# Hybrid decoder layer on one core: two moving operands of gate and up in memory of their own, decode columns kept in SBUF, output projection's tiles in shared buffers

## The chip, the cores and the metric

The kernel runs on one core of one Trainium2 chip. The metric is the device time of one execution in microseconds. The core has a matrix engine (PE), a vector engine (DVE), a scalar engine (ACT), a general engine (POOL) and a sequencer that issues DMAs (SP). Each engine works through its own list of instructions in order, and waits at an instruction until what it needs is there. POOL issues DMAs too.

## The reference

One inference step of one layer with 2048 prompt rows and 8 decode rows of width 1024. Two head groups (sliding-window attention and gated linear attention) give `mix`; then come the output projection, an RMS norm and a gated feed-forward layer:

```python
D_MODEL, SEQ, DEC_BATCH = 1024, 2048, 8
D_FF = 2816

def rmsnorm(x, g):
    r = lax.rsqrt(jnp.mean(x * x, axis=-1, keepdims=True) + EPS)
    return x * r * g

def finish(x, o_attn, o_gla, r_gla, ...):
    ...
    h = x + jnp.concatenate([o_attn, g], axis=-1) @ w_o
    z = rmsnorm(h, ffn_norm_g)
    return h + (jax.nn.silu(z @ w_gate) * (z @ w_up)) @ w_down
```

`finish` is called for the prompt rows and for the decode rows. All is float32.

## The kernel before

A float32 matrix is held as two halves, high and low, each of a type that PE multiplies at full rate. `split` (L91) makes them: a copy to the rounded type on ACT (L92), and the rest by a subtraction on DVE (L93). `mm3` (L102) multiplies two split matrices with three matmuls (L104, L105, L106), high by high, high by low, low by high.

The program runs through these stages:

- Projections, attention and gated linear attention, up to about 765 us. The last blocks of linear attention (L800 to L889) store `mix_d` blocks from SP (L889) and the final state (L948). The change doesn't touch this code.
- The output projection, from about 740 to 947 us (L963 to L1080). It goes over sixteen tiles of 128 prompt rows and then the eight decode rows. The prompt has two halves of 1024 rows, 0 and 1 (`sb`), with eight tiles each; a pair of tiles 4 apart belongs together (`mt` 0 to 3), so the order is 0, 4, 1, 5, 2, 6, 3, 7, 8, 12, 9, 13, 10, 14, 11, 15, decode.
- Gate and up, in two passes over the weights, one for each half of the prompt (959 to 1403 and 1403 to 1847 us). Each pass goes over eleven pairs of weight blocks of 256 columns.
- The down projection, from 1853 us to the end (L1246 to L1347).

For a tile, `load_tile` fetches the tile of `mix_d` (`mr`, L995) and of x (`h`, L1000), and splits `mr` into `mt`. `product` multiplies by the two halves of W_o, `WO0` and `WO1` (48 matmuls into `ps_wo`), adds to h on DVE (`add_h`, L580), and stores h (L1022) for the end of the layer. `normalise` follows one tile later: Square with a sum on ACT (L1030), the root (L111 on DVE, L112 on POOL), the scaled z on DVE (L1032), eight transposes on PE (`ps_zT`, L1037), and the copies of the result into four tiles b11, b21, b12, b22 (L1040). When a pair of tiles is done, `operands` builds the seven moving operands of Strassen's scheme (in Winograd's form) from them: four differences on DVE (L958), seven splits (`zhl`, a ring of three buffers), and seven stores from POOL into DRAM, `zc_d` (L1057). The scheme replaces eight block products with seven, P1 to P7.

The eight decode rows ride along as four extra columns (eight rows in two blocks of four) on the last pair, (half 1, `mt` 3): their normed rows are copied into columns 128 to 131 of that pair's b tiles (L1043), so its operands are 132 columns per block wide and can be built only when the decode rows have been through the output projection. In half 1 the moving operands are therefore 516 wide, and a unit of products is run in two pieces of 258.

Gate and up take the seven operands of a half as z0 to z6, loaded on SP (L1242), in the order P1, P6, P2, P7, P5, P4, P3 (`PRODS`). The tiles of all seven lie in one pool that is opened when the output projection's pools are closed. For each pair of weight blocks the raw weights come from DRAM (`wrg`, L1179), sums and differences of blocks are made on DVE (L958, L961: `sx`, `sy`), and the results are split (`whl`). A unit is one product for gate or up: twelve matmuls of 128x512 in half 0. Their results meet in `ps_a` (P1, P2), `ps_b` (P6, P7, P4) and `ps_c` (P5, P3). At the end of a pair the result's seven operands for the down stage go to DRAM from POOL (`md_d`, L1236).

What sets the order: the program is written in Python, and before it is built, a scheduler that simulates the engines chooses for each engine the order of its instructions, among those that dependencies and buffers allow. Pools are stacks of memory; a tile that is opened over a closed one waits until the older tiles' last users are done.

## Time and profile before

| | us |
|---|---|
| runs shown, median (lowest to highest) | 2315.32 (2309.81 to 2316.54) |
| the profiled execution | 2311.51 |
| its span in the trace | 2309.7 |
| PE busy in the span | 2227.1 |
| last product of a prompt tile with W_o ends | about 937.8 |
| first product of gate and up begins | 959.10 |
| first P5 product of gate and up begins | 996.34 |

Times in the profile are counted from the start of the span. A line of the timeline gives the start, the duration, the engine, the kernel's line, the operation with its output and input tiles, and in brackets how long the engine stood idle before it and for what. A line of the waits view gives an engine's waits by cause: total, number and the longest. A line of the windows view gives for a stretch its length, each engine's busy time with its number of instructions in the order PE, PEld, DVE, ACT, POOL, then the clock granted to PE, the DMA engines' busy share, and GB/s.

### The profile page before, as it was taken

To read this page: it belongs to the slowest core of one execution; us is meant where nothing else is said; L and a number is where in the kernel's file an instruction comes from. 1 tells how busy PE (TensorE), PEld (TensorE's weight loads), DVE (VectorE), ACT (ScalarE), POOL (GpSimd) and SP (SyncE) were. 2 spreads that over 40 slices of the span, in tenths; PEclk is the share of its full clock that TensorE was granted. 3 is DMA by queue.
4 is the path that set the end of the run, shared out by engine and by line. 5 is a ranking of instruction groups with operands and counts; after the bars stand their busy time and mean duration, and the time that the engine had idled before them with its cause. 6 is when DMAs were issued, how large, how long until landed. Compare 5 with 4: busy or idle time off the path is not lost.

```text
span 2309.7 us, 34809 instructions
## 1 busy us (share of the span) xinstructions
PE 2227.1 (96%) x12649; PEld 1923.6 (83%) x12649; DVE 1600.5 (69%) x3236; ACT 957.2 (41%) x2120; POOL 623.8 (27%) x791
## 2 busy tenths in 40 slices
PE   8999998999999999699999999999999989999998
PEld 6888886788887788578888889999999968787887
DVE  6787887587776567556666666767676674847477
ACT  5676777343443234323232333333333243535342
POOL 2443434365465133201111110101010122222222
PEclk9999998999998999899999999999999999999999
DMA  7323234245325689872324257323233277878877
GB/s 239 122 75 115 93 108 153 90 157 165 126 87 214 225 275 288 276 247 87 119 79 127 78 177 290 110 84 115 87 111 97 83 225 171 210 165 213 185 184 263
DMA packets 204935, 364.57 MB, mean 158 GB/s; under 512 B 15411, under 2 KB 128332, under 8 KB 200780
## 3 DMA queue, kind: packets, MB, share of 16 engines
q1 hardware_dynamic: 167740, 258.80, 34.2%
q0 software_dynamic: 37024, 103.55, 17.9%
q8 instruction: 100, 1.64, 0.3%
q14 instruction: 71, 0.58, 0.1%
HBM read 211.09 MB, written 152.27 MB: 157 GB/s over the span
## 4 chain that ended last, share of the span: by engine, by line
PE 31%; issue 20%; POOL 5%; DMA 1%; DVE 0%; POOLq 0%; ACT 0%; SPq 0%; DVEq 0%; ACTq 0%
PE ps_b L105 4%; PE ps_b L104 4%; PE ps_b L106 4%; POOL h_d L1329 4%; PE ps_c L105 3%; PE ps_c L104 3%; PE ps_c L106 3%; PE ps_a L105 3%; PE ps_a L106 3%; PE ps_a L104 3%; POOL out_y_prompt_dram L1324 1%; DMA z<-zc_d_P 1%; POOL md_d L1236 1%; DMA zc_d_P<-zhl 0%; DMA wrg<-in_w_gate_dram 0%
## 5 line engine op out<-in xcount | busy, mean ns | idle before, releaser
L104 PE MATMUL ps_b<-z,whl 128*128 128x258 f32 (+1 forms) x792 | 253.8, 321 | 3.2 <-DMA z<-zc_d_P 3.2
L105 PE MATMUL ps_b<-z,whl 128*128 128x258 f32 (+1 forms) x792 | 254.0, 321 | 0.0
L106 PE MATMUL ps_b<-z,whl 128*128 128x258 f32 (+1 forms) x792 | 252.8, 319 | 0.0
L92 ACT CAST dm<-mr 128x384 fp32r<-128x384 f32 (+1 forms) x224 | 108.0, 488 | 188.4 <-PE ps_b L106 97.6
L104 PE MATMUL ps_a<-z,whl 128*128 128x258 f32 (+1 forms) x528 | 170.9, 324 | 8.3 <-DMA z<-zc_d_P 8.3
L105 PE MATMUL ps_a<-z,whl 128*128 128x258 f32 (+1 forms) x528 | 170.7, 323 | 0.0
L106 PE MATMUL ps_a<-z,whl 128*128 128x258 f32 (+1 forms) x528 | 170.3, 323 | 0.0
L104 PE MATMUL ps_c<-z,whl 128*128 128x258 f32 (+1 forms) x528 | 168.6, 319 | 0.9 <-DMA z<-zc_d_P 0.9
L105 PE MATMUL ps_c<-z,whl 128*128 128x258 f32 (+1 forms) x528 | 169.1, 320 | 0.0
L106 PE MATMUL ps_c<-z,whl 128*128 128x258 f32 (+1 forms) x528 | 168.9, 320 | 0.0
L104 PEld LDWEIGHTS ps_b<-z,whl 128*128 128x128 f32 x792 | 149.3, 189 | 15.9 <-DMA z<-zc_d_P 3.5
L106 PEld LDWEIGHTS ps_b<-z,whl 128*128 128x128 f32 x792 | 149.2, 188 | 12.1
L105 PEld LDWEIGHTS ps_b<-z,whl 128*128 128x128 f32 x792 | 149.2, 188 | 11.9
L93 DVE TENSOR_TENSOR dm<-mr,dm 128x384 fp32r<-128x384 f32 (+1 forms) x224 | 114.9, 519 | 59.4 <-ACT dm L92 59.4
L92 ACT CAST whl<-wrg 128x512 fp32r<-128x512 f32 x132 | 81.6, 620 | 150.5 <-PE ps_b L106 81.2
L802 POOL TENSOR_TENSOR bd<-E,qTb 64x128 f32<-64x128 f32 x224 | 127.1, 567 | 60.6 <-ACT E L787 47.2
L93 DVE TENSOR_TENSOR whl<-wrg,whl 128x512 fp32r<-128x512 f32 x132 | 90.9, 688 | 42.9 <-ACT whl L92 42.7
L961 DVE TENSOR_TENSOR gu<-ps_c,gu 128x512 f32<-128x512 f32 (+1 forms) x130 | 77.9, 600 | 61.0 <-PE ps_c L106 60.3
L1236 POOL DMA_DIRECT2D md_d<-m x22 | 15.7, 713 | 373.7 <-DVE m L1199 360.3
L104 PEld LDWEIGHTS ps_a<-z,whl 128*128 128x128 f32 x528 | 100.8, 191 | 17.0 <-issue 4.4
L104 PEld LDWEIGHTS ps_c<-z,whl 128*128 128x128 f32 x528 | 99.8, 189 | 9.3 <-ACT whl L92 1.3
L105 PEld LDWEIGHTS ps_a<-z,whl 128*128 128x128 f32 x528 | 100.5, 190 | 8.2
(385 smaller groups left out, 6625.9 us busy)
## 6 DMA issues: line engine op xcount, KB each, us to landing
mr<-md_d SPq DMA_DIRECT2D x24, 1344.0 KB
zc_d_P<-zhl POOLq DMA_DIRECT2D x49, 512.0 KB, 6.1
wrg<-in_w_gate_dram SPq DMA_DIRECT2D x44, 512.0 KB
wrg<-in_w_up_dram SPq DMA_DIRECT2D x44, 512.0 KB
nT_d<-nT SPq DMA_DIRECT2D x16, 1024.0 KB
zT<-nT_d SPq DMA_DIRECT2D x8, 2048.0 KB
z<-zc_d_P SPq DMA_DIRECT2D x7, 2064.0 KB
z<-zc_d_P SPq DMA_DIRECT2D x7, 2048.0 KB
```

What stands on the lines that cost most here:

```text
L92: nc.scalar.copy(h, src)
L93: (eng or nc.vector).tensor_tensor(l, src, h.bitcast(F32), ALU.subtract)
L104: nc.tensor.matmul(ps, lh, rh, start=start, stop=False, skip_group_check=more)
L105: nc.tensor.matmul(ps, lh, rl, start=False, stop=False, skip_group_check=more)
L106: nc.tensor.matmul(ps, ll, rh, start=False, stop=stop, skip_group_check=more)
L802: nc.gpsimd.tensor_tensor(bv[rows, :, h], eo, qo, ALU.mult)
L961: nc.vector.tensor_tensor(out, a, b, ALU.add)
L1236: nc.gpsimd.dma_start(md_d[sb][g][:, :, q, fp - GROUPS[g][0], :], src.rearrange("p (m t) -> p m t", m=4))
L1324: nc.gpsimd.dma_start(O["y_prompt"][0, ti * P:(ti + 1) * P, cols], hq[which])
L1329: nc.gpsimd.dma_start(h_d[ti][:, cols], c, accum_op=ALU.add)
```

## The change

Memory is laid out anew around the output projection:

- z0 and z1 (P1 and P6) get pools of their own, opened before the output projection. z2 and z3 lie over WO0, z4 and z5 over WO1, z6 over the `mt` tiles; for this each half of W_o has a pool of its own, padded.
- To make room, h tiles come from the ring of seven buffers `cu` that later holds the weight splits (`whl`), the differences t1 to t4 from `csum`, the pool that later holds weight sums; z, b11 to b22 are single instead of double; the first two `mr` tiles use the memory of z0 and z1.
- The decode rows no longer ride on the last pair's DRAM operands. They are normed into a small tile `zd`, their seven operands are built in it by the same differences (`sums_z`), and split into `zdec` in SBUF. In half 1 seven copies on POOL (L1275) put them into columns 512 to 515 of z0 to z6, whose loads now bring 512 columns. `operands` of the last pair follows tile 15. Four of its seven splits use two `mt` buffers (`zhl2`) beside the ring of three.
- The decode rows' h is stored from POOL instead of SP (L1032).
- The pool of gate and up's results is divided in two, with the same number of buffers.

```diff
+    zdec = pool(ctx, "c_zdec", 1).tile([P, 7, 2, 16], F32R, name="zdec")
...
+    zph = ctx.enter_context(ExitStack())
+    zpools = {q: pool(zph, f"g_z{q}", 1, side="right") for q in (0, 1)}
+
+    def ztile(q, name):
+        return zpools[q].tile([P, 2, 4, 516], F32R, tag="z", name=name)
...
+        wops = [pool(ph, f"m_wo{dh}", 1, side="right") for dh in range(2)]
         mixp = pool(ph, "m_mix", 2, side="right")
-        wop = pool(ph, "m_wo", 1, side="right")
         hlp = pool(ph, "m_hl", 3, side="right")
-        hp = pool(ph, "m_h", 3, side="right")
-        zp = pool(ph, "m_z", 2, side="right")
+        zp = pool(ph, "m_z", 1, side="right")
         bp = pool(ph, "m_b", 1, side="right")
-        tp = pool(ph, "m_t", 1, side="right")
...
-            h = hp.tile([P, D], F32, tag="h", name="h")
+            h = cu.tile([P, D], F32, tag="hl", name="h")
...
-                mr = hlp.tile([P, 1056], F32, tag="hl", name="mr")[:, :1024]
+                mr = ztile(tiles.index(ti), "mr").rearrange("p s k t -> p (s k t)")[:, :1024].bitcast(F32)
...
-            nc.sync.dma_start(h_d[ti] if ti < NB else hdec_d, h[:n])
+            if ti < NB:
+                nc.sync.dma_start(h_d[ti], h)
+            else:
+                nc.gpsimd.dma_start(hdec_d, h[:n])
...
+            t = [csum.tile([P, 512], F32, tag="s", name=f"t{i}").rearrange("p (k t) -> p k t", k=4) for i in range(4)]
+            sums_z(b, t)
+            spare = []
+            for q, src in enumerate((b11, t[1], b21, t[2], t[0], t[3], b22)):
+                if (sb, mt) == (1, 3) and q >= 3:
+
+                    if not spare:
+                        two = mixp.tile([P, 2 * KD * P + 16], F32R, tag="mix", name="zhl2")[:, :2 * KD * P]
+                        spare = [x for x in two.rearrange("p (i s k t) -> i p s k t", i=2, s=2, k=4)]
+                    hl = spare.pop(0)
+                else:
+                    hl = hlp.tile([P, 2, 4, P], F32R, tag="hl", name="zhl")
+                split(hl[:, 0], hl[:, 1], src)
+                nc.gpsimd.dma_start(zc_d[sb][q][:, :, :, mt * P:mt * P + P], hl.bitcast(F32))
...
             if ti == NB:
-                normalise(ti, hs.pop(ti), [x[:, :, P:P + 4] for x in bs[1, 3]])
-                operands(1, 3, bs.pop((1, 3)))
+
+                d = bp.tile([P, 8, 4, 4], F32, name="zd")
+                b = [d[:, i] for i in (0, 2, 7, 6)]
+                normalise(ti, hs.pop(ti), b)
+                sums_z(b, [d[:, i] for i in (4, 1, 3, 5)])
+                split(zdec[:, :, 0], zdec[:, :, 1], d[:, 0:7].rearrange("p q k t -> p q (k t)"))
                 return
...
-            if j == 1 and (sb, mt) != (1, 3):
+            if j == 1:
                 operands(sb, mt, bs.pop((sb, mt)))
...
-                bs[ti // 8, ti % 4] = [bp.tile([P, 4, 132], F32, tag=f"b{q}", name=f"b{q}", bufs=2) for q in range(4)]
+                bs[ti // 8, ti % 4] = [bp.tile([P, 4, P], F32, tag=f"b{q}", name=f"b{q}") for q in range(4)]
...
-        zcp = pool(ph, "g_zc", 1, side="right")
+        for q in range(2, 7):
+            zpools[q] = pool(ph, f"g_z{q}", 1, side="right")
...
-            zc = {name: zcp.tile([P, 2, 4, 516], F32R, tag=f"z{q}", name=f"z{q}")[:, :, :, :WIDTHS[sb]]
-                  for q, name in reversed(list(enumerate(PRODS)))}
+            zc = {name: ztile(q, f"z{q}") for q, name in enumerate(PRODS)}
             for q, name in enumerate(PRODS):
-                nc.sync.dma_start(zc[name].bitcast(F32), zc_d[sb][q])
+                nc.sync.dma_start(zc[name][:, :, :, 0:512].bitcast(F32), zc_d[sb][q])
+                if sb == 1:
+                    nc.gpsimd.tensor_copy(zc[name][:, :, :, 512:516],
+                                          zdec[:, q].bitcast(F32).rearrange("p s (k t) -> p s k t", k=4))
```

How this moves instructions is shown at three places. A row has the line, the operation, the output and input tiles (the number behind a name tells its instances apart) and the shape; "x4" counts equal rows. In lines of the changed kernel L1212 is the weight load, L1273 the z load, L1030 the store of h.

SP's list from the end of the output projection on, before: seven z loads in a row behind the store of the decode rows, and weight loads of the second pair behind them.

```order
L1022 DMA h_d11_4834<-h_9762 128x1024
L1179 DMA wrg_10473<-in_w_gate_dram 128x4x256
L1022 DMA h_d15_4838<-h_9846 128x1024
L1022 DMA hdec_d_4839<-h_9962 8x1024
L1242 DMA z0_10184<-zc_d0_P1_4840 128x8x512
L1242 DMA z1_10183<-zc_d0_P6_4841 128x8x512
L1242 DMA z2_10182<-zc_d0_P2_4842 128x8x512
```

SP's list of the changed kernel, from the store of tile 8's h on, and again from that of tile 15's on:

```order
L1030 DMA h_d8_4831<-h_9169 128x1024
L1273 DMA z0_10204<-zc_d0_P1_4840 128x8x512
L1002 DMA mr_9770<-mix_d11_84 128x1024
L1007 DMA h_9853<-in_x_prompt_dram 128x1024
L1030 DMA h_d12_4835<-h_9253 128x1024
L1273 DMA z1_10205<-zc_d0_P6_4841 128x8x512
```

```order
L1030 DMA h_d15_4838<-h_9853 128x1024
L1273 DMA z2_10206<-zc_d0_P2_4842 128x8x512
L1273 DMA z3_10207<-zc_d0_P7_4843 128x8x512
L1273 DMA z4_10208<-zc_d0_P5_4844 128x8x512
L1273 DMA z5_10209<-zc_d0_P4_4845 128x8x512
L1212 DMA wrg_10499<-in_w_gate_dram 128x4x256
```

z0 stands eight prompt tiles earlier, behind the store of tile 8, and z1 behind that of tile 12; z2 to z5 stand behind the store of tile 15 and no longer behind that of the decode rows.

ACT's list around the Square of tile 15, before. The tiles `zhl` are splits of the operands of the pair of tiles 10 and 14, `whl` are weight splits of the first pair of gate and up, and z_10076 belongs to tile 15.

```order
L92 CAST whl_10266<-sy_10263 128x512
L92 CAST whl_10283<-wrg_10201 128x512
L92 CAST whl_10299<-wrg_10205 128x512
L92 CAST whl_10315<-sx_10241 128x512
L1040 COPY b3_9645<-ps_zT_9920 128x4x128
L1030 ACTIVATE z_10017,ss_10018<-h_9762 128x1024
L92 CAST zhl_9938<-t1_9927 128x4x128
L92 CAST zhl_9942<-b1_9643 128x4x128
L92 CAST zhl_9946<-t2_9928 128x4x128
L92 CAST zhl_9950<-t0_9926 128x4x128
L1030 ACTIVATE z_10076,ss_10077<-h_9846 128x1024
```

ACT's list at the same place in the changed kernel, where z_10083 belongs to tile 15, z_10138 to the decode rows, and zhl_10111 and zhl2_10123 to the operands of the last pair:

```order
L92 CAST zhl_9953<-t2_9935 128x512
L92 CAST zhl_9957<-t0_9933 128x512
L92 CAST zhl_9961<-t3_9936 128x512
L92 CAST zhl_9965<-b3_9652 128x512
L1051 COPY b1_9850<-ps_zT_10038 128x512
L1041 ACTIVATE z_10083,ss_10084<-h_9853 128x1024
L92 CAST zhl_10111<-b0_9849 128x512
L1051 COPY b3_9852<-ps_zT_10097 128x512
L1041 ACTIVATE z_10138,ss_10139<-h_9969 8x1024
L92 CAST zhl2_10123<-t0_10103 128x512
```

The Square of tile 15 stands behind all seven splits of the pair before, not behind five of them, and only two weight splits stand ahead of it (whl_10233 and whl_10250, further up in the list) instead of seven. On PE the decode rows' transposes, which stood ahead of the first product of gate and up, stand behind its first 24 (the two units of P1).

SP's list at the start of the output projection in the changed kernel (h_8493, h_8509 and h_8569 are the x tiles 0, 4 and 1; mr_8570 is the mix tile 1):

```order
L948 DMA out_gla_state_prompt_dram<-Sbd_4981 64x128 x4
L889 DMA mix_d15_88<-mob_8412 128x512
L1007 DMA h_8493<-in_x_prompt_dram 128x1024
L1007 DMA h_8509<-in_x_prompt_dram 128x1024
L1002 DMA mr_8570<-mix_d1_74 128x1024
L1007 DMA h_8569<-in_x_prompt_dram 128x1024
```

Before, the x tiles 0, 4 and 1 stood ahead of the state's stores, and the mix tile 1 stood right behind the last mix store (L889). Correspondingly DVE adds `ps_wo` to the first two tiles (four additions) only behind the last work of the linear attention, ahead of the scaled z of tile 0.

More of the change, by code (lines that the diff above doesn't have):

```diff
@@ L1043, in normalise, with sums_z @@
                         nc.vector.tensor_copy(bs[2 * j + hf], pv[:, :, 4 * j:4 * j + 4])
-        def operands(sb, mt, b):
-            w = 132 if (sb, mt) == (1, 3) else P
-            b11, b21, b12, b22 = (x[:, :, :w] for x in b)
-            t1, t2, t3, t4 = (tp.tile([P, 4, 132], F32, tag=f"t{i}", name=f"t{i}")[:, :, :w] for i in range(4))
+        def sums_z(b, t):
+            b11, b21, b12, b22 = b
+            t1, t2, t3, t4 = t
             sub(t1, b12, b11)
@@ L1080, in hymba_kernel, with out @@
         after(tiles[-1])
-    cy = pool(ctx, "c_out", 2)
+    cy1, cy2 = pool(ctx, "c_out1", 2), pool(ctx, "c_out2", 2)
+    def out(tag, name):
+        return (cy2 if tag in ("gu3", "uu2", "uu3") else cy1).tile([P, 516], F32, tag=tag, name=name)
     def units(parts, sums):
@@ L1134, in __init__ @@
             self.pp, self.pieces, self.done = ppool, pieces, done
-            self.p1, self.u2, self.u3 = (cy.tile([P, 516], F32, tag=tag + x, name=tag + x) for x in ("p1", "u2", "u3"))
+            self.p1, self.u2, self.u3 = (out(tag + x, tag + x) for x in ("p1", "u2", "u3"))
             self.banks = {}
```

29 lines of the change are left out of this document (14 added, 15 removed).

## The prediction

> **What bounds the kernel now.** I read the page first, for the engine that is busy throughout.
>
> ```profile
> PE 2227.1 (96%) x12649; PEld 1923.6 (83%) x12649; DVE 1600.5 (69%) x3236; ACT 957.2 (41%) x2120; POOL 623.8 (27%) x791
> PE   8999998999999999699999999999999989999998
> ```
>
> TensorE is busy for 96% of the span, and the change removes none of its products: it can only win idle time of PE, or matmuls at half clock. The row of tenths has one hole worth the name, the seventeenth slice, which reads 6 (16 to 17 fortieths of 2309.7: 924 to 982 us). So I read next what PE waited for.
>
> ```profile
> PE ps_zT L1037 <- DVE z L1032: 6.9, 1, 6.9
> PE ps_a L104 <- DMA z<-zc_d_P: 8.3, 2, 4.3
> PE ps_b L104 <- DMA z<-zc_d_P: 3.2, 2, 3.0
> PE ps_c L104 <- DMA z<-zc_d_P: 0.9, 1, 0.9
> PE ps_wo L104 <- ACT mt L92: 4.2, 2, 3.0
> ```
>
> The first four lie at one place, the step from the output projection to gate and up: 6.9+8.3+3.2+0.9 = 19.3 us of idle time. One is for the decode rows' norm (z of L1032), the others for the moving operands z0 to z6 out of DRAM. The last line is the start of the output projection. The windows of 10 us show the hole with its clock (after the engines: PEclk, DMA share, GB/s):
>
> ```profile
> 930.00:940.00 10.00, 10.00 (x50) 7.91 (x49) 7.97 (x13) 2.24 (x6) 3.43 (x4) 1.00 0.60 184
> 950.00:960.00 10.00, 1.89 (x10) 1.73 (x11) 6.57 (x14) 2.94 (x5) 2.43 (x4) 0.56 0.84 297
> 960.00:970.00 10.00, 7.60 (x23) 5.59 (x22) 1.37 (x2) 1.26 (x2) 1.56 (x2) 0.75 1.03 328
> ...
> 1000.00:1010.00 10.00, 10.00 (x45) 8.09 (x44) 2.41 (x5) 1.85 (x3) 0.71 (x1) 1.00 1.02 358
> ```
>
> PE is full up to 940 and again from 1000. Between them it stands, and where it runs the clock is down, to 0.56 and 0.75 of full speed, while the DMA share is over 1: the transfers set the pace. The timeline gives the order of events:
>
> ```profile
> 945.90 1.03 PE L1037 MATMUL ps_zT<-ident,z 128*128 128x128 f32 x8
> 950.34 0.29 SPq L1022 DMA_DIRECT2D hdec_d<-h  x1
> 950.81 40.70 SPq L1242 DMA_DIRECT2D z<-zc_d_P  x7
> 953.83 0.99 PE L1037 MATMUL ps_zT<-ident,z 8*128 8x8 f32 x8 [6.90 <-DVE z L1032]
> 959.10 0.80 PE L104 MATMUL ps_a<-z,whl 128*128 128x512 f32 x1 [4.28 <-DMA z<-zc_d_P]
> 964.81 0.46 PE L105 MATMUL ps_a<-z,whl 128*128 128x512 f32 x1
> 965.34 0.40 PE L104 MATMUL ps_a<-z,whl 128*128 128x512 f32 x1
> 967.20 0.40 PE L106 MATMUL ps_a<-z,whl 128*128 128x512 f32 x1
> 970.62 0.51 PE L104 MATMUL ps_b<-z,whl 128*128 128x512 f32 x1 [3.02 <-DMA z<-zc_d_P]
> 982.03 0.76 PE L104 MATMUL ps_a<-z,whl 128*128 128x512 f32 x1 [4.03 <-DMA z<-zc_d_P]
> 996.34 0.47 PE L104 MATMUL ps_c<-z,whl 128*128 128x512 f32 x1 [0.93 <-DMA z<-zc_d_P]
> ```
>
> The seven loads (2 MB each) start only at 950.8, behind the decode rows' store on SP, and PE meets z0, z1, z2 and z4 before they are there. At full clock a product starts every 0.2325 us (965.34 to 967.20, eight steps); after the wait of 4.28 it is 0.43 (from 959.10 thirteen steps to 964.81, 0.44 on the mean). From the end of tile 15's transposes (946.93) to the first P5 product at 996.34 are 49.4 us. The work in them is the decode transposes, 0.99, and eight units of twelve products (P1, P6, P2, P7, gate and up), 96 × 0.2325 = 22.3. So **26 us are lost here**: some 19 idle, the rest half clock. Nothing else in the profile is open to this change.
>
> **The change, part by part.** (1) *The step to gate and up.* z0 and z1 are loaded when the first two tiles of half 1 (8 and 12) are done, tens of us before they are wanted, and z2 to z5 as soon as the last products with each half of W_o are done (942 and 946, by the decode products that end at 946.0), no longer behind the decode norm. The decode transposes move behind the 24 P1 products. All seven z waits should go. What is late next is the chain that feeds it. Its rows of before:
>
> ```profile
> 938.39 7.67 PE L1019 MATMUL ps_wo<-WO,mixdec 128*40 128x512 f32 x32
> 939.92 0.62 ACT L92 CAST zhl<-t 128x512 fp32r<-128x512 f32 x1 [5.80 <-DMA zc_d_P<-zhl]
> 940.45 1.05 ACT L1030 ACTIVATE z<-h 128x1024 f32<-128x1024 f32 x1
> 944.30 1.28 DVE L1032 SCALAR_TENSOR_TENSOR z<-h,rs_r,gBf 128x1024 f32<-128x1024 f32 x1
> 945.64 0.62 ACT L92 CAST zhl<-b 128x512 fp32r<-128x512 f32 x1 [1.99 <-DMA zc_d_P<-zhl]
> 952.41 1.27 DVE L1032 SCALAR_TENSOR_TENSOR z<-h,rs_r,gBf 8x1024 f32<-8x1024 f32 x1 [0.74 <-POOL rs_r L112]
> ACT zhl L92 <- DMA zc_d_P<-zhl: 70.1, 26, 6.6
> ```
>
> and, from the page's groups, what one split of weights takes on ACT and on DVE:
>
> ```profile
> L92 ACT CAST whl<-wrg 128x512 fp32r<-128x512 f32 x132 | 81.6, 620 | 150.5 <-PE ps_b L106 81.2
> L93 DVE TENSOR_TENSOR whl<-wrg,whl 128x512 fp32r<-128x512 f32 x132 | 90.9, 688 | 42.9 <-ACT whl L92 42.7
> ```
>
> In the new ACT order the Square of tile 15 (940.45 before) stands behind all seven splits of the pair before, of which the last ran at 945.64 because three buffers turn with the stores' landing. So Square starts near 946.3; from Square to the transposes took 945.90 − 940.45 = 5.45 us, of which some 1.5 was queueing on DVE and POOL: I take 950.1 for the transposes, **4.2 us of idle time that was not there**. The 24 P1 products then run to about 957. The decode norm starts after the copy of tile 15's b (951.7); its Square, rstd and z take what they took before (from 950.34, when the rows were complete, to 953.68, 3.3 us), and on DVE four differences, one weight sum and two splits of 0.7 stand among them: transposes at about 960, **some 3 us idle**. Then P6 needs its weight split, which in the new DVE order comes behind the decode copies and all splits of tile 15's operands; of the fourteen weight splits of the first pair only two are made ahead (before, the four in the ACT rows of the last section as well, and the three ahead of them). At 0.62 (ACT) and 0.69 (DVE) each (the last two rows) I make it ready at 964 to 965: **4 to 5 us idle**. From there DVE (sums and splits, some 1.4 us a unit) is faster than PE (2.8 a unit), and z6 is not wanted before P3. Sum of idle: 4.2+3+4.5 = 11.7. Half clock after waits of this length: before, 13 products at 0.44 after 4.28 us is 13 × 0.2 = 2.7 us lost. Two such spells would be 5, but what is lost while a feeder is late is no loss of its own: I take 2 to 3. Left: 14 of 26. **Gain 12 us**, bounds 5 (every wait half as long again, 20 idle and half clock) and 20 (only the first wait of 4.2 left, with its half clock).
>
> On the clock the Trainium skill (TensorE: Matmul & The Clock Gate, Part 1: The HAM clock gate) says that an idle window of about 3.4 us throttles PE to half, and that about 3.4 us of work free it. The trace agrees for the 4.28 us wait (half clock for 5.7 us). By that rule the wait of 3 us might go free and the two others cost about 1.7 each, 3.4 together instead of my 2 to 3.
>
> (2) *Start of the output projection.* The first h tiles come from a ring that still holds other things, so in the new SP order their loads stand behind the mix store of the last block, and ahead of the second pair's mr.
>
> ```profile
> 765.26 0.32 SPq L889 DMA_DIRECT2D mix_d<-mob  x1
> 765.69 2.50 SPq L995 DMA_DIRECT2D mr<-mix_d  x3
> 767.76 1.04 PE L1037 MATMUL ps_zT<-ident,z 128*128 128x128 f32 x8
> 771.82 0.50 PE L104 MATMUL ps_wo<-WO,mt 128*128 128x512 f32 x1 [3.02 <-ACT mt L92]
> ...
> PE ps_wo L106 <- DVE mt L93: 1.1, 1, 1.1
> ```
>
> Before, tile 0's transposes ran at 767.76, in a gap; now h lands after about 768, four adds of 0.69, Square, rstd and z follow, and the transposes come at about 773.5, but into the wait for mt that PE has anyway (771.82), shifted by the two loads' issue, 0.7. I take **+1**. Bounds: −1 (the 1.1 us wait for the low half of mt goes, since its split now stands ahead of the block's own work) and +5 (an h load takes the 6.1 us that mr took from 765.69 to the product, and then the adds).
>
> (3) *The output projection's stream.* z0 and z1 put 4 MB more on the DMA engines between some 870 and 930.
>
> ```profile
> 780.00:940.00 160.00, 160.00 (x759) 132.97 (x758) 107.77 (x162) 60.71 (x101) 47.61 (x58) 1.00 0.86 268
> ```
>
> PE has no idle time in these 160 us, at a DMA share of 0.86; 4.2 MB at the 358 GB/s of the window from 1000 take 11.7 us of 60, against 0.14 × 60 = 8.4 free. So the stores of the operands land a little later, and with them the splits (their waits stand above, 70.1 us in 26). Single instead of double b, z and difference tiles hang on the same splits: b22 is free after the last of seven, some 7 × 2.9 (939.92 to 945.64, two steps) = 20 us into a pair of tiles, which takes PE 2 × 12.1 = 24 (48 products at 0.23 and the transposes, 1.03). **+0.5**, bounds 0 and +5.
>
> (4) *The rest at 0.* Seven POOL copies of decode columns (high and low halves of 16 columns) lie between md_d stores on an engine that is busy for 27%. Only the second piece of a unit needs its copy; bounds 0 and +3, if a copy waits for its z and holds a store. Loads of 2 KB runs at the start of half 1: PE has no gap there.
>
> ```profile
> 1390.00:1400.00 10.00, 10.00 (x45) 8.09 (x44) 8.47 (x14) 3.50 (x6) 0.71 (x1) 1.00 1.01 428
> ```
>
> The operands of the last pair are now 512 wide, not 528, and no longer wait for the decode rows: in part 1. The down stage loads its first operands after the last gate product as before.
>
> **Sum:** −12 + 1 + 0.5 = −10.5 on the profiled execution's 2311.5 (span 2309.7 and 1.8 around it): 2301. That execution lies 3.8 below the median of the runs shown and 1.7 above the lowest, so I put the median at **2302**.
>
> **Rivals.** *All of it* (0.20): the chain keeps up, because splits and sums fill ACT and DVE idle time (DVE is busy 6.6 and 1.4 of 10 us in the windows at 950 and 960); only tile 15's late transposes stay: −20 + 1, about 2293 (with the 1 us of the median). *The stall changes its name* (0.20): PE waits as long for whl, the decode z and tile 15's z as it did for the loads; the two weights ready ahead speak for it, the six that were ready before against it. 20 of the 26 stay: −6 + 2, about 2309. Here too belongs the case that the loads of z2 to z5 do not come early, their memory being that of W_o. *Slower* (0.08): the ring of three split buffers becomes the bound of the output projection. It decides when a pair's seven splits take longer than PE's 24 us, that is at 3.4 us a split; they stand at 2.9. The loads of z0 and z1 reach the pairs of half 1, and the single b tiles pass the delay on to PE. At 4.3 us a split, half as long again, it is 30 − 24 = 6 us in each of three pairs, 18 on top of the forecast: about 2320.
>
> The Trainium skill (DMA: Bandwidth & Descriptors, Issuing engines are not separate DMA queues) holds that all queues end in the same 16 engines and interleave. That speaks for this rival: a share of 0.86 leaves the early loads no bandwidth of their own, whichever queue they are on.
>
> **Chances.** Forecast 0.52 (2296 to 2307), all 0.20, renamed 0.20, slower 0.08. A run can tell about 0.3%, 7 us, from no change: faster takes the forecast, less its edge, and all of the first rival: 0.69; within: 0.22; slower: 0.09, with the upper bounds of parts 2 and 4. The range is 2288 to 2314: it leaves out the slower case, and a little at each end.
>
> **What would show it.** In the profile after: no wait of PE for z loads by DMA; the transposes of tile 15 with a wait of about 4 us on z; the first P6 product waiting for whl on ACT or DVE; first P5 product some 12 us earlier against the last decode product; PE 10.00 in every window of the output projection. It is wrong if waits for z loads stay (then SP's queue is held ahead of them), if PE shows gaps between 870 and 940 (the ring), or if the boundary near 1390 has one (POOL's copies).

## The result and the profile after

| | before | after |
|---|---|---|
| median of the runs, us (lowest to highest) | 2315.32 (2307.68 to 2319.19, 5 runs) | 2301.44 (2299.76 to 2301.97, 5 runs) |
| ratio after to before | | 0.9945 [0.9933, 0.9958] |
| profiled execution / its span | 2311.51 / 2309.7 | 2301.44 / 2299.7 |
| A: first decode product with W_o | 938.4 | 945.1 |
| from A to B, the last product of gate and up (L104) | 908.1 | 889.3 |
| from B to C, the last product of the down stage (L104) | 455.6 | 453.6 |
| from C to the end of the span | 7.6 | 11.7 |

Faster by 0.5%, and 2302 was forecast. The four lower rows show that the sum came out by terms that were each off. The step is worth 18.8 us, not 12; the program reaches the step 6.7 us later, not 1.5; the last 4.1 us were in no term. −18.8 + 6.7 − 2.0 + 4.1 = −10.0, the difference of the spans.

The page after, in its lines of PE and of the 40 slices: the hole of the seventeenth slice (6 before) is gone.

```profile
PE 2223.9 (97%) x12649; PEld 1921.5 (84%) x12649; DVE 1597.5 (69%) x3241; ACT 955.6 (42%) x2121; POOL 627.8 (27%) x799
PE   8999998899998899999999999999999999999997
```

PE's waits after, between 765 and 1025 us, are these five. Of the 12.4 us in which PE waited at the step for z to be loaded, 0.2 is left, and of the 6.9 for the decode rows' norm 1.8; two short waits for weight splits are new, and the wait for `mt` at the start of the output projection has grown from 4.2 in two to 6.9 in one:

```profile
PE ps_wo L104 <- ACT mt L92: 6.9, 1, 6.9
PE ps_zT L1048 <- DVE z L1043: 1.8, 1, 1.8
PE ps_b L106 <- DVE whl L93: 1.7, 1, 1.7
PE ps_b L104 <- ACT whl L92: 1.2, 1, 1.2
PE ps_c L104 <- DMA z<-zc_d_P: 0.2, 1, 0.2
```

The window from A to 1010 us, of before, and that with the next of after (length, then busy time with the number of instructions of PE, PEld, DVE, ACT, POOL, then PEclk, DMA share, GB/s):

```profile
938.40:1010.00 71.60, 52.22 (x206) 38.61 (x205) 28.38 (x48) 18.69 (x31) 11.59 (x15) 0.86 0.99 332
```

```profile
945.10:1010.00 64.90, 59.95 (x258) 45.33 (x257) 48.80 (x84) 26.34 (x47) 13.58 (x15) 0.95 0.89 312
1010.00:1400.00 390.00, 390.00 (x1715) 316.99 (x1714) 261.67 (x406) 120.05 (x201) 55.19 (x81) 1.00 0.41 130
```

Behind 1010 PE is full at full clock, as it was before from 1000: the gain lies at the step alone. Up to 1010 PE stood for 71.60 − 52.22 = 19.4 us before and for 64.90 − 59.95 = 5.0 after. That is 14.4 of the 18.8; the other 4.4 are put down to matmuls that no longer run at half clock. Of the 26 us that the prediction counted as lost, 7.2 remain: 5.0 idle and 2.2 by the clock.

The timeline of after shows the step:

```profile
945.12 7.65 PE L1026 MATMUL ps_wo<-WO,mixdec 128*40 128x512 f32 x32
945.98 0.62 ACT L92 CAST zhl<-b 128x512 fp32r<-128x512 f32 x1 [0.47 <-DMA zc_d_P<-zhl]
949.09 22.82 SPq L1273 DMA_DIRECT2D z<-zc_d_P  x4
952.60 1.04 PE L1048 MATMUL ps_zT<-ident,z 128*128 128x128 f32 x8
953.40 0.47 PE L104 MATMUL ps_a<-z,whl 128*128 128x512 f32 x1
961.04 0.66 PE L1048 MATMUL ps_zT<-ident,z 8*128 8x8 f32 x8 [1.83 <-DVE z L1043]
962.22 0.62 ACT L92 CAST whl<-sy 128x512 fp32r<-128x512 f32 x1 [3.13 <-DVE sy L966]
962.89 0.66 PE L104 MATMUL ps_b<-z,whl 128*128 128x512 f32 x1 [1.20 <-ACT whl L92]
965.70 0.79 PE L106 MATMUL ps_b<-z,whl 128*128 128x512 f32 x1 [1.72 <-DVE whl L93]
981.53 0.47 PE L104 MATMUL ps_c<-z,whl 128*128 128x512 f32 x1 [0.22 <-DMA z<-zc_d_P]
```

The transposes of tile 15 follow the decode products with no wait (945.12 + 7.65), and the first product of gate and up starts at 953.40. The first P5 product at 981.53 has one unit fewer ahead of it than before (P7 of up now comes behind it), so it isn't compared with 996.34; the stretch from A to B is.

### The profile page after: what moved, and what is told of

It reads as the page before. It is cut to its first block, busy times and chain, and to the rows that moved or that the text cites. A ratio compares the mean times of both kernels' runs of the same rounds, so it can differ in the third digit from the quotient of the medians.

```text
span 2299.7 us, 34866 instructions
## 1 busy us (share of the span) xinstructions
PE 2223.9 (97%) x12649; PEld 1921.5 (84%) x12649; DVE 1597.5 (69%) x3241; ACT 955.6 (42%) x2121; POOL 627.8 (27%) x799
## 4 chain that ended last, share of the span: by engine, by line
PE 81%; DVE 5%; DMA 5%; issue 4%; POOL 2%; ACT 2%; SPq 0%; POOLq 0%; DVEq 0%; ACTq 0%
PE ps_b L105 7%; PE ps_b L104 7%; PE ps_b L106 7%; PE ps_c L105 5%; PE ps_c L104 5%; PE ps_c L106 5%; PE ps_a L105 5%; PE ps_a L104 5%; PE ps_a L106 5%; PE ps_d L104 3%; PE ps_wo L104 3%; PE ps_d L106 3%; PE ps_d L105 3%; PE ps_wo L106 3%; PE ps_wo L105 3%
## 5 line engine op out<-in xcount | busy, mean ns | idle before, releaser
L104 PE MATMUL ps_b<-z,whl 128*128 128x258 f32 (+1 forms) x792 | 254.0, 321 | 1.2 <-ACT whl L92 1.2
L104 PE MATMUL ps_c<-z,whl 128*128 128x258 f32 (+1 forms) x528 | 168.6, 319 | 0.2 <-DMA z<-zc_d_P 0.2
L104 PE MATMUL ps_a<-z,whl 128*128 128x258 f32 (+1 forms) x528 | 168.8, 320 | 0.0
L104 PEld LDWEIGHTS ps_b<-z,whl 128*128 128x128 f32 x792 | 149.4, 189 | 13.1 <-ACT whl L92 1.3
L92 ACT CAST whl<-sy 128x512 fp32r<-128x512 f32 x88 | 54.6, 620 | 134.7 <-PE ps_b L106 84.7
L104 PE MATMUL ps_wo<-WO,mt 128*128 128x512 f32 x256 | 103.6, 404 | 6.9 <-ACT mt L92 6.9
L104 PEld LDWEIGHTS ps_c<-z,whl 128*128 128x128 f32 x528 | 99.8, 189 | 8.6 <-issue 0.6
```

Source lines behind the costliest of these rows:

```text
L92: nc.scalar.copy(h, src)
L104: nc.tensor.matmul(ps, lh, rh, start=start, stop=False, skip_group_check=more)
```

## The experiments

All times are medians, ratios are to the kernel before on the same chip (medians there 2314.92 for the first four, 2314.47 for the next four, 2315.03 for the last three). Stretches come from each run's own profile.

| run | us | ratio | A | A to B | B to C | C to end |
|---|---|---|---|---|---|---|
| again | 2300.72 | 0.9938 [0.9925, 0.9952] | 941.9 | 889.4 | 455.2 | 11.7 |
| h_first | 2295.91 | 0.992 [0.9906, 0.9933] | 938.4 | 889.3 | 453.7 | 11.7 |
| dec_only | 2314.65 | 1.0002 [0.9993, 1.001] | 944.6 | 903.1 | 454.7 | 11.7 |
| mem_only | 2317.79 | 1.0014 [1.0004, 1.0023] | 946.2 | 908.9 | 453.8 | 11.7 |
| no_spare | 2312.39 | 0.999 [0.9981, 0.9999] | 943.9 | 901.9 | 453.9 | 11.7 |
| mem_spare | 2303.95 | 0.995 [0.9937, 0.9962] | 941.1 | 896.3 | 453.8 | 11.7 |
| hoist | 2300.54 | 0.9934 [0.9922, 0.9947] | 939.8 | 892.5 | 454.7 | 11.7 |
| hdec_sp | 2297.47 | 0.9925 [0.9913, 0.9938] | 937.2 | 893.9 | 455.5 | 7.7 |
| pad | 2293.74 | 0.9901 [0.9886, 0.9916] | 936.0 | 891.9 | 454.7 | 11.7 |
| z6_late | 2309.4 | 0.9973 [0.9962, 0.9984] | 940.8 | 899.5 | 454.5 | 11.7 |
| pad_y | 2295.43 | 0.9914 [0.9901, 0.9927] | 938.1 | 889.6 | 455.6 | 11.6 |

*again* is the changed kernel on the chip of the first four, the yardstick for them.

> The changed kernel once more, on the chip of the three runs beside it, as their yardstick. All theories: 2299 to 2303 us, last product of the decode rows with W_o starting near 945, first P5 product near 981.5.

Its stretch is that of the first profile within 0.1; its A lies 3.2 us earlier, and B to C is 1.6 longer. So A and B to C move by some us from one execution to the next. The stretch from A to B is steadier, but not always to the microsecond: *pad* and *pad_y* below have the same order on PE, ACT and DVE up to the down stage, and their stretches are 891.9 and 889.6. A difference of some 2 to 3 us between two stretches is therefore not read as an effect.

**h_first: the late h loads undone.** h of tiles 0, 4, 1 and 5 lies in the part of z0's and z1's memory that `mr` leaves free, not in the ring of weight splits.

```diff
+            if ti in tiles[:2]:
+                zt = ztile(tiles.index(ti), "mr").rearrange("p s k t -> p (s k t)").bitcast(F32)
+                early[tiles[tiles.index(ti) + 2]] = zt[:, 2048:3072]
+                h = zt[:, 1024:2048]
+            elif ti in early:
+                h = early.pop(ti)
+            else:
+                h = cu.tile([P, D], F32, tag="hl", name="h")
```

> The changed kernel, with the x tiles (h) of tiles 0, 4, 1 and 5 in the free part of the memory of z0 and z1, so that their loads no longer wait for the weight ring's memory. Theory (late h loads cost 5 to 6 us at the start of the output projection, and everything behind moves as one): PE's 6.9 us wait for mt falls to about 3, decode products start 5 us earlier, near 940, and the time is about 2296 us. Rival 1 (the late start comes from the order of mr, not of h): no change, 2300 or more. Rival 2 (the step to gate and up takes back what the start gains, since the splits' ring and the loads then come too late): decode products earlier by 5 us, first P5 product by less than 2, time 2299 or more.

The timeline around the first products, of after and then of h_first. In after, DVE waits 10.28 us for the h load, whose issue (766.93) stands behind the mix store (766.39), and the splits of `mt` stand behind its adds; in h_first the last of the same four adds (h of tiles 0 and 4 is named `mr` there) comes at 765.42 and waits for its product, not for a load:

```profile
766.39 0.33 SPq L889 DMA_DIRECT2D mix_d<-mob  x1
766.93 0.85 SPq L1007 DMA_DIRECT2D h<-in_x_prompt_dram  x2
771.81 2.48 DVE L580 TENSOR_TENSOR h<-ps_wo,h 128x512 f32<-128x512 f32 x4 [10.28 <-DMA h<-in_x_prompt_dram]
775.32 0.79 PE L104 MATMUL ps_wo<-WO,mt 128*128 128x512 f32 x1 [6.93 <-ACT mt L92]
```

```profile
765.42 0.69 DVE L580 TENSOR_TENSOR mr<-ps_wo,mr 128x512 f32<-128x512 f32 x1 [4.81 <-PE ps_wo L106]
769.43 0.80 PE L104 MATMUL ps_wo<-WO,mt 128*128 128x512 f32 x1 [3.17 <-ACT mt L92]
```

The wait is 3.2 instead of 6.8 (again), A is 3.5 earlier, the stretch unchanged, the median 4.8 lower. The theory holds in kind; the late loads cost 3 to 4 us, not the 5 to 6 that it had. This version's median is the lower one, but the intervals of the two ratios overlap a little.

**dec_only: decode columns alone.** z0 to z6 are opened together when W_o is done with (z0 and z1 over its memory), h has a pool of its own, and the decode part and the spare buffers stay.

```diff
-    zpools = {q: pool(zph, f"g_z{q}", 1, side="right") for q in (0, 1)}
+    zpools = {}
...
-        for q in range(2, 7):
+        for q in range(7):
```

> Decode columns in SBUF as in the changed kernel, but z0 and z1 loaded over the memory of W_o like the others, and h and the first mr tiles in buffers of their own as before. Theory (the early loads carry most of the gain, since 14 MB from 946 on at 330 to 390 GB/s end near 985): PE waits for z by DMA 8 to 10 us again, against 5 us won at the start: about 2304 us. Rival (it is enough that the loads no longer stand behind the decode rows' norm and store): waits for z under 2 us, about 2296 us.

A wait of PE, and two rows of its timeline with another:

```profile
PE ps_b L104 <- DMA z<-zc_d_P: 2.9, 1, 2.9
```

```profile
948.54 20.09 SPq L1274 DMA_DIRECT2D z<-zc_d_P  x4
962.10 0.76 PE L104 MATMUL ps_a<-z,whl 128*128 128x512 f32 x1 [9.00 <-DMA z<-zc_d_P]
```

The loads are issued 4.0 us behind A instead of 12.4, and yet z0 is there only 13.6 us after its issue, when before it took 8.3 (950.81 to 959.10). PE waits for the loads as it did. The stretch is 5.0 shorter than before, which a later A takes back: no gain. A is 6.2 later though h has a pool of its own here, so late h loads aren't the only thing that delays A; at the start of the output projection PE waits 3.17 and 1.82 us for `mt`, and the granted clock from 770 to 780 is 0.71, where before it is 1.00.

**mem_only: memory alone.** Buffers as after, but the decode columns ride on the last pair's operands through DRAM, as before, and all splits go through the ring of three.

```diff
-                if (sb, mt) == (1, 3) and q >= 3:
...
-                        two = mixp.tile([P, 2 * KD * P + 16], F32R, tag="mix", name="zhl2")[:, :2 * KD * P]
...
-            normalise(ti, hs.pop(ti), bs[sb, mt][2 * j:2 * j + 2])
-            if j == 1:
+            normalise(ti, hs.pop(ti), [x[:, :, :P] for x in bs[sb, mt][2 * j:2 * j + 2]])
+            if j == 1 and (sb, mt) != (1, 3):
```

> Memory as in the changed kernel (z0 and z1 early, shared buffers), but the decode columns ride on the last pair's operands through DRAM as before. Theory (the early loads carry the gain): within 3 us of the changed kernel, 2300 to 2305 us. Rival (the decode columns carry it, because the last pair's splits and the loads behind them come later): 2308 us or more, with PE waits for whl or z over 8 us at the step.

The loads of z0 and z1 are early and PE still waits, now for whl. Both waits for whl stand in these rows of its timeline (9.7 us together); a third wait, of 4.3, is for `uu`:

```profile
969.80 0.80 PE L104 MATMUL ps_b<-z,whl 128*128 128x512 f32 x1 [6.53 <-ACT whl L92]
977.25 0.63 ACT L92 CAST zhl<-t 128x528 fp32r<-128x528 f32 x1 [3.25 <-DMA zc_d_P<-zhl]
977.78 0.61 ACT L92 CAST whl<-sy 128x512 fp32r<-128x512 f32 x1
978.45 0.63 PE L104 MATMUL ps_b<-z,whl 128*128 128x512 f32 x1 [3.16 <-ACT whl L92]
```

The weight split at 977.78 stands in ACT's list behind a split that waits 3.25 us for a ring buffer, that is for a store to land. The longer wait, 6.53, isn't the ring's: ACT makes that split at 969.13, as soon as DVE has made its `sy` (968.41), which stands in DVE's list behind the copies of the decode rows and the last pair's differences. Early memory alone is worth nothing (908.9 against 908.1): this is the rival "the stall changes its name".

**no_spare: the changed kernel without the two spare buffers.**

```diff
-                if (sb, mt) == (1, 3) and q >= 3:
+                if False:
```

> The changed kernel, with all seven splits of the last pair in the ring of three buffers (no zhl2). Measure: from the first decode product with W_o to the last ps_c product of gate and up (before 908.1, changed kernel 889.3, mem_only 908.9). Theory (what holds mem_only back is that ring splits wait on ACT for stores that share the DMA engines with the z loads, with the weight splits queued behind them; the spare buffers are half of the remedy): waits of PE for whl 3 to 8 us, stretch 893 to 898, time 2305 to 2310 us. Rival (the decode rows' lateness alone is the cause, the ring is not): stretch 889 to 891, time 2299 to 2303 us.

Three rows of its timeline:

```profile
943.33 0.53 SPq L1273 DMA_DIRECT2D z<-zc_d_P  x1
947.90 22.18 SPq L1273 DMA_DIRECT2D z<-zc_d_P  x4
978.87 0.77 PE L104 MATMUL ps_c<-z,whl 128*128 128x512 f32 x1 [9.00 <-DMA z<-zc_d_P]
```

Of the 18.8 us of the stretch 12.6 are lost again (901.9), but not where the theory had them: the waits for whl stay at 0.8 and 0.7. The `mt` memory is free earlier, so z6, wanted last, is loaded first (943.33) ahead of z2 to z5; and the scheduler has put P5 (z4) ahead of P2 and P7, so PE meets z4 before it has landed. Of PE's other waits there, one of 2.2 us is for `gp`, which ACT copies out of `ps_a`.

**z6_late** parts these two: no_spare with the decode rows' h in an `mt` buffer, so that z6 comes behind z2 to z5 again.

```diff
+            if ti == NB:
+                h = mixp.tile([P, 2 * KD * P + 16], F32R, tag="mix", name="h")[:, :D].bitcast(F32)
+            else:
+                h = cu.tile([P, D], F32, tag="hl", name="h")
```

> no_spare, with the decode rows' x in an mt buffer, so that z6's memory comes free only after the decode norm and its load is issued behind z2 to z5 as in the changed kernel. Theory (no_spare lost through the loads: z6, wanted last, was issued first, and PE's order took P5 of z4 third): PE's wait for z4 falls from 9.0 to 3 to 5 us, time 2305 to 2309 us. Rival 1 (the ring's waits in front of the weight splits cost it): the wait moves to whl, 2311 or more. Rival 2 (z6's place is all of it): no wait for z over 1 us, 2300 to 2303 us.

The same rows of its timeline:

```profile
944.80 19.81 SPq L1276 DMA_DIRECT2D z<-zc_d_P  x4
973.28 0.77 PE L104 MATMUL ps_c<-z,whl 128*128 128x512 f32 x1 [5.32 <-DMA z<-zc_d_P]
```

The wait for z4 falls from 9.0 to 5.3, a little less than expected, the stretch by 2.4, the median by 3. The place of z6 may be worth about 3 us, but the edit also takes the decode rows' h out of the ring of weight splits, and 2.4 us of the stretch is hardly more than pad and pad_y differ by. P5 still comes at 973.28, ahead of P2 and P7, and waits; that the rest of the 12.6 is this order was not tried by itself.

**mem_spare: mem_only with the spare buffers** for the last four splits (in `mt` buffers of 2112 words).

```diff
+                if (sb, mt) == (1, 3) and q >= 3:
+                    if not spare:
+                        two = mixp.tile([P, 2112], F32R, tag="mix", name="zhl2")
+                        spare = [x for x in two.rearrange("p (i s k t) -> i p s k t", i=2, s=2, k=4)]
+                    hl = spare.pop(0)
```

> mem_only (decode columns ride on the last pair through DRAM) with the spare buffers for four of the last pair's splits. Theory (ring waits in front of the weight splits): PE's waits for whl fall from 9.7 to 4 to 6 us, stretch 898 to 903, time 2308 to 2312 us. Rival (the decode rows' lateness): within 2 us of mem_only, 2316 or more.

Its longest wait for whl at the step (two others are 0.8 and 0.6):

```profile
PE ps_b L104 <- ACT whl L92: 8.4, 1, 8.4
```

2303.95 is below what either theory gave. The waits for whl haven't fallen in sum (9.7 us, as in mem_only), so the theory's account of them is wrong: the 8.4 ends on a `sy` of DVE, as the 6.53 of mem_only does. What is gone is the wait of 3.16 behind the ring and the 4.3 for `uu`; and z6 is loaded last, where mem_only, like no_spare, issues one load (945.63) ahead of the other four. Early memory and spare buffers together give 908.1 − 896.3 = 11.8 of the 18.8. The columns in SBUF add the rest: 896.3 − 889.3 = 7.0. Some of these come back ahead of A, where the wider `mt` buffers of mem_spare help (below): in the medians the two kernels are 3 us apart.

**hoist: h_first with the first four weight splits ahead.** The remaining waits at the step are for whl, so the splits of P1 and P6 are requested ahead of tile 15's norm and operands.

```diff
             hs[ti] = product(ti, *now)
+            if i == len(tiles) - 1:
+                first[:] = load_w(w_g, 0), load_w(w_u, 0)
+                first.append([next(u) for u in (first[0], first[1], first[0], first[1])])
```

> h_first, and in the program the first four weight splits (P1 and P6, gate and up) are asked for ahead of tile 15's norm and operands. Theory (what is left of the stall, 1.2 + 2.1 us for whl and the half clock behind it, is the place of the P6 splits in the queues): no waits for whl over 0.5 us, PE's clock 1.00 in the windows from 950 to 980, stretch 884 to 886 instead of 889.3, time about 2292 us. Rival (the splits ahead delay tile 15's norm and the operand ring, and PE waits for z of L1091 instead): a wait for z of 3 us or more, time 2295 us or more.

Its waits of PE at the step, and two of its windows:

```profile
PE ps_a L105 <- ACT gp L1205: 2.4, 1, 2.4
PE ps_b L105 <- DMA z<-zc_d_P: 2.1, 1, 2.1
PE ps_c L105 <- DMA z<-zc_d_P: 2.0, 1, 2.0
```

```profile
950.00:960.00 10.00, 10.00 (x49) 7.83 (x48) 9.54 (x20) 4.70 (x10) 4.40 (x5) 1.00 1.03 396
960.00:970.00 10.00, 6.13 (x26) 4.43 (x24) 5.30 (x13) 5.27 (x9) 2.17 (x3) 1.00 1.03 394
```

The waits for whl are gone, and PE is full to 960. Then it waits for `gp`, a copy on ACT, and twice for z, at a DMA share of over 1 and 395 GB/s. The step has a second floor close below the first: PE gets to the operands sooner than the four loads have landed. Neither theory nor rival had this. The median, 2300.54, lies above h_first's, with intervals of the ratios that overlap, and the stretch is 3.2 longer.

**pad: h_first with `mt` buffers of 64 words of padding instead of 16.** In the changed kernel a tile of the output projection takes longer than before, without a gap. The time from one tile's transposes to the next is 11.77 to 11.82 before and 11.87 and 12.03 in turn after; in mem_spare, the run with wider `mt` buffers, it is 11.77.

```diff
-            mt = mixp.tile([P, 2 * KD * P + 16], F32R, tag="mix", name="mt")[:, :2 * KD * P]
+            mt = mixp.tile([P, 2 * KD * P + 64], F32R, tag="mix", name="mt")[:, :2 * KD * P]
...
-                d = bp.tile([P, 8, 4, 4], F32, name="zd")
+                d = csum.tile([P, 512], F32, tag="s", name="zd")[:, :128].rearrange("p (q k t) -> p q k t", q=8, k=4)
```

> h_first, with the mt buffers padded by 64 words again as in the kernel before, not by 16 (the small tile zd moves into the ring of weight sums to make room). Theory (the pad alone sets the pace of the output projection: 11.80 us a tile before, 11.87 and 12.03 in turn in every kernel with a pad of 16, 11.77 in mem_spare with 64): 11.77 to 11.80 a tile, 2 to 2.7 us earlier at the decode products, time about 2293.5 us. Rival (the single b and z tiles set it): pace and time as h_first, 2295 to 2297 us.

The transposes of two tiles in h_first, and the same in pad:

```profile
794.20 1.04 PE L1057 MATMUL ps_zT<-ident,z 128*128 128x128 f32 x8
806.21 1.04 PE L1057 MATMUL ps_zT<-ident,z 128*128 128x128 f32 x8
```

```profile
793.94 1.04 PE L1057 MATMUL ps_zT<-ident,z 128*128 128x128 f32 x8
805.71 1.03 PE L1057 MATMUL ps_zT<-ident,z 128*128 128x128 f32 x8
```

12.01 and 11.77: the padding sets the pace, as it does between mem_only and mem_spare, and A is 2.4 us earlier. At the step PE waits 4.0 for whl (1.2 and 2.1 in h_first): the splits don't come sooner because PE does. Whether the step takes the gain back can't be told. The stretch is 2.6 longer than h_first's in pad and 0.3 in pad_y, which has the same order on PE, ACT and DVE up to there and a wait for whl of 4.1. The two executions differ in the granted clock behind that wait; the window from 954 to 964 in pad, then in pad_y:

```profile
954.00:964.00 10.00, 5.88 (x14) 4.12 (x14) 9.97 (x25) 4.51 (x9) 3.46 (x4) 0.50 1.04 395
```

```profile
954.00:964.00 10.00, 5.76 (x18) 4.11 (x18) 9.97 (x25) 4.58 (x9) 3.46 (x4) 0.66 1.04 396
```

The median of pad, 2293.74, is the lowest here, but that of pad_y is 2295.43 and that of h_first 2295.91, and the intervals of their ratios overlap, so a gain in time from the padding isn't shown.

**hdec_sp and pad_y: the end of the program.** All kernels with the decode rows' h stored from POOL end 11.6 to 11.7 us after the last down product, the kernel before 7.6.

```diff
-                nc.gpsimd.dma_start(hdec_d, h[:n])
+                nc.sync.dma_start(hdec_d, h[:n])
```

> h_first, with the decode rows' h stored from SP again, behind the loads of z2 to z5. Theory (with the loads ahead of it, the queue of this store doesn't matter): within 1 us of h_first, 2295 to 2297 us, and the 11.7 us from the last matmul to the end of the span (7.6 before) stay. Rival (the store on POOL is what lengthens the end): 7.6 us there, about 2292 us.

Two rows of its timeline:

```profile
962.19 7.33 SPq L1041 DMA_DIRECT2D hdec_d<-h  x1
979.02 0.62 ACT L92 CAST whl<-wrg 128x512 fp32r<-128x512 f32 x1 [9.77 <-DMA hdec_d<-h]
```

The end is 7.7 with the store on SP, so the 4 us hang on it. They are not gained: on SP the store stands behind four z loads (962.19), the h it reads holds a buffer of the weight splits' ring, and ACT waits 9.77 us for that buffer. The stretch grows by 4.6. pad_y, pad with one store of y on SP instead of POOL, asks whether the number of POOL's DMAs matters:

```diff
+                        eng = nc.sync if (ti, dh) == (0, 0) else nc.gpsimd
+                        eng.dma_start(O["y_prompt"][0, ti * P:(ti + 1) * P, cols], hq[which])
```

> pad, and one early store of y of the down stage's last group issued from SP instead of POOL, PE's order being the same. Theory (the end is longer by 4.1 us wherever POOL issues one DMA more than in the kernel before: 11.7 us from the last matmul to the end in eight kernels, 7.6 and 7.7 in before and hdec_sp): 7.6 us there, time about 2289.5 us. Rival (it is the decode rows' store from POOL itself, not the count): 11.7 us, time as pad.

It does not: 11.6, at 2295.43. The two rows are the last stores from POOL, of after and of before:

```profile
2290.56 0.54 POOL L1359 DMA_DIRECT2D out_y_prompt_dram<-hq  x1 [0.82 <-DVE hq L969]
```

```profile
2304.67 0.54 POOL L1324 DMA_DIRECT2D out_y_prompt_dram<-hq  x1 [0.82 <-DVE hq L961]
```

From there to the end of the span are 9.1 us after and 5.0 before. The last data land about 2.6 and 2.2 us behind these rows; the rest shows no instruction. Why a store of 32 KB from POOL, 1300 us earlier, lengthens it stays open.

## Why the prediction was right, and where it was not

- **What bounds the kernel:** right. The loss was at the step, none of PE's products went, and behind 1010 us PE is full in both.
- **Part 1, the step: right in kind, too small.** −18.8 against −12 (bounds 5 and 20): what happened lies near the rival "all of it". The term that was mis-sized is "what is late next", 11.7 us of idle time that measured 5.0. Tile 15's transposes: 4.2 forecast, 0 measured. The decode transposes: 3, measured 1.83. The weight split of P6: 4.5, measured 1.20 + 1.72. The half clock: 2 to 3, measured 2.2. The upper bound of 20 kept the wait of tile 15 and dropped the others; it came the other way round. One reading of before was off as well: the half clock that the prediction puts down to the wait of 4.28 us is granted from 951.27 us on, inside the wait of 6.90 for the decode rows' norm.
- **The step of it that failed** is "the last ran at 945.64 because three buffers turn with the stores' landing. So Square starts near 946.3". The order was right, the time was carried over from before. Against the decode products, the last split ran 945.64 − 938.39 = 7.25 us behind their start before, and 945.98 − 945.12 = 0.86 after (1.3 in h_first, whose A is that of before). The rows of the two traces show why in part. Before, four weight splits stand on ACT between the previous pair's splits and this pair's, at 924.96 to 926.53; after, none. By the rows it is on DVE that they hold this pair up. Before, six weight instructions stand there without a wait but one of 0.69 us, from 924.25 to 928.63, ahead of the add to h that ACT's next Square waits for, and this pair's differences come behind it. After, DVE stands idle for 2.45 us before the same add, waiting for PE. The add in before, then in after:

```profile
928.63 0.68 DVE L580 TENSOR_TENSOR h<-ps_wo,h 128x512 f32<-128x512 f32 x1
```

```profile
932.65 0.69 DVE L580 TENSOR_TENSOR h<-ps_wo,h 128x512 f32<-128x512 f32 x1 [2.45 <-PE ps_wo L106]
```

  The first split of the pair runs 3.7 us earlier against the decode products. The other 2.7 us lie behind the pair's third split, where the waits for landing sum to 8.75 before and 7.57 after. That the weight splits are the cause was read from the lists and not tried. A split that the change moves away from a queue is a gain for those behind it, and I had counted only those that are missing later.
- **What makes the gain**, by the runs: not one part. Memory alone makes the stretch 0.8 longer; the decode part with the spare buffers makes it 5.0 shorter, memory with the spare buffers 11.8, memory with the decode part 6.2 (no_spare), all three 18.8. The prediction had put the gain down to the loads and taken the rest off it as a remainder. I read this as loads that wait for memory, splits that wait for the ring, and the decode norm standing in series, each hiding the others. It is not parted cleanly: the spare buffers alone and the decode part alone weren't run, in no_spare the order of the loads and of P5 changes too, and mem_spare has wider `mt` buffers.
- **Part 2, the h loads: +1 forecast (−1 to +5), 3 to 4 measured** by undoing it. The mechanism was the one named as the bound ("an h load takes the 6.1 us that mr took"), taken too low: PE's existing wait was supposed to hide it, but the `mt` splits that this wait is for stand behind the h adds.
- **Part 3, the stream: +0.5 forecast, about 2 measured, by another cause.** The ring did not become the bound: PE has no gap from 780 to 940. A tile takes 11.95 us on the mean instead of 11.8 with PE busy throughout, and pad shows that the `mt` buffers' size does it.
- **A in all:** +6.7. Of it 1.5 arises at 350 to 364 us, in code that the change doesn't touch (again has A 3.2 earlier, so such drift is part of the measurement); 3 to 4 are part 2 and 2 are part 3.
- **Part 4, at 0:** POOL's copies and the boundary cost nothing in PE's waits (PE is busy for all of the 434 us from 1400 to 1834). What was not in any part is the end, +4.1 us, from the one edit that looked free, the decode store on POOL.
- **The time was right by luck**, because the errors cancel: the step gave 6.8 more than forecast and the down stage 2.0 (within what again shows), A took 5.2 more than its 1.5, and the end 4.1. That is 0.5 in all: −10.0 against −10.5.
- **The rivals:** "renamed" is what mem_only does, "slower" does not occur in any run.

## What to carry to other kernels

Memory that is freed earlier lets a load start earlier only for what lies there, so what is wanted last should lie where memory comes free last: z6 ahead of z2 to z5 came with about 3 us here. This stall, with several feeders behind one another (loads, the ring of splits, the decode norm), yielded nothing when memory alone was freed and most when all were, so undo the parts both ways before a gain is credited to one. Run the same order of instructions twice before a difference of 2 or 3 us in one profile is called an effect. When a step is forecast from the trace of before, carry its queue along relative to the product that it feeds, and list what leaves the queue as well as what enters it.

## What the hardware showed that was not expected

- **The clock falls after short waits too.** In after, matmuls of up to 0.79 us follow the waits of 1.83, 1.20 and 1.72 us at the step. Narrow windows show that the clock fell before the third of these (963.98 to 965.70), so the third had no part in it:

```profile
959.67:963.08 3.41, 0.84 (x9) 0.76 (x10) 3.37 (x5) 0.62 (x1) 2.54 (x4) 1.00 1.05 397
963.08:969.90 6.82, 5.10 (x12) 3.50 (x12) 6.79 (x19) 3.62 (x8) 2.56 (x3) 0.50 1.04 395
```

  In the 3.41 us before the fall PE was busy for 0.84 us, 0.66 of them the eight small decode transposes. The windows are 3.41 us long because the steps of the granted clock in this trace lie multiples of that apart (771.93, 778.76, 963.08 and 969.90 us). Before, the wait of 3.02 us that ends at 771.82 left the clock full. Counted back in such steps from the fall at 951.27 of that trace, the wait lies across two windows, and PE was busy for more than half of each:

```profile
766.97:770.38 3.41, 1.82 (x13) 1.38 (x11) 1.44 (x3) 1.70 (x4) 0.28 (x1) 1.00 0.81 239
770.38:773.79 3.41, 1.97 (x12) 1.61 (x12) 3.02 (x3) 1.39 (x2) 1.17 (x2) 1.00 0.90 286
```

  The Trainium skill (TensorE: Matmul & The Clock Gate, Part 1: The HAM clock gate) gives an idle window of about 3.4 us. The trace agrees on the length, but the window before the fall was not wholly idle. How much work keeps the clock up can't be told from these rows; no run tries it. The rows of after also show DVE busy for 3.37 of 3.41 and 6.79 of 6.82 us: it is the engine that the waits for whl end on.
- **The padding of the stationary operand's buffer (`mt`) changes the pace of its matmuls**, 48 words by 0.1 to 0.26 us a tile, with no gap to be seen. Why isn't shown, nor whether it is the place of `mt` itself or of the tiles behind it in memory.
- **A load that is issued earlier isn't there earlier by as much.** z0 of dec_only took 13.6 us from issue to the end of PE's wait, that of before 8.3; which other traffic it shared the engines with was not looked into. Loads issued within a few us came one behind another: before, PE's waits for z0, z1 and z2 end at 959.10, 970.62 and 982.03; in dec_only those for z0 and z1 at 962.10 and 972.87. With the DMA share over 1 the traffic in the windows quoted here is 394 to 397 GB/s, but 328 and 358 in those of before that the prediction shows (from 960 and from 1000).
- **A small store from POOL in mid-program came with 4 us at the end**, in every kernel that had it and in neither that had it on SP.
